# A rule for the order of TensorE's matmuls in a planned kernel: groups that begin whole, and wide runs of at least nine

## The chip, the cores and the metric

The kernel runs on one core of one Trainium2 chip. The metric is the device time of one execution in microseconds (us), median of three runs. The core has a matrix engine (TensorE, PE in the profile; its weight loads are listed as PEld), VectorE (DVE), ScalarE (ACT), GpSimd (POOL) and SyncE (SP), which issues DMAs. Each engine works through its own queue in the order that the program gave it and waits on semaphores for what other engines or DMAs deliver.

## The reference

One decoder layer over 2048 positions of width 1024:

```
h = rms_norm(x, mix_norm_pre)
m = hybrid_mixer(h, ...)                 # attention heads + gated recurrence, then w_out
x = x + rms_norm(m, mix_norm_post)
h = rms_norm(x, mlp_norm_pre)
x = x + rms_norm(squared_relu_mlp(h, w_ff_in, w_ff_out), mlp_norm_post)
```

The attention has 8 heads of 64 columns. Each query attends to three dilated windows, (128, 1), (512, 4) and (2048, 16), and their outputs are weighted by their softmax denominators. The MLP is `relu(h @ w1)**2 @ w2` with a hidden width of 4096. All inputs and outputs are float32.

## The kernel before

**Halves.** The positions are worked on in two halves of 1024. Half 0 goes through projections, first attention, output projection, MLP-in and MLP-out, and half 1 follows. The two overlap in one place that matters here: the attention of half 1 (`attention(..., 1, ...)`, "second attention") runs together with the MLP-out of half 0. The function `interleave` (line 1399) writes the two into one program: between the steps of the attention it puts steps of the MLP-out (`fill`, line 1405), each step three matmuls.

**The MLP-out** (`mlp_out`, line 1183) is a block product in seven partial products `m` (Strassen's scheme), each over 16 blocks `j` and 4 row tiles `t`. Every float32 factor is split into a high and a low part, so a product is three matmuls of 512 columns each (lines 1234 to 1236) into a PSUM tile whose name begins with `o0_` (half 0) or `o1_` (half 1). Their factors come by DMA and are split on ACT and DVE (`part`, line 1310) a few blocks ahead.

**The second attention** (`attention`, line 380) has 48 parts: 8 heads, for each of which two parts A (line 541, the near window) and four parts B (line 601, the dilated ones). A part has three steps, which use PSUM tiles of three kinds:

- scores, twice per part: matmuls into `S1_...` (part A, two query blocks, two matmuls each of 256 columns, line 569) or `SB1_...` (part B, two matmuls of 384 or 512 columns, lines 626 and 627). DVE adds the mask and takes the row minimum (line 426), ACT takes the exponential (line 432).
- turn, twice per part: three or four transposes of 128x128 blocks into `pT1_...` (line 405); ACT and DVE split the result into high and low (lines 56 and 57).
- values: ten matmuls into `oA1_...` (line 593) or eight into `oB1_...` (line 652), of 256 and 128 columns; ACT and DVE fold the result (lines 420 and 421).

At the end of each pair of heads `join` (line 670) weights the two sums: 18 small matmuls into `pst1_...` (lines 684 and 686), then DVE, and stores and loads through DRAM (lines 705, 712, 737). The stores to `smix` feed the output projection of half 1 (tile `m`, lines 869 to 871).

**PSUM** has eight banks; in the second attention the scores share two (`B`), the transposes and the values share two (`T`), and MLP-out holds four (`A` and `O`).

**What sets the order.** The program is traced in the order written, and then `Plan.run` (line 1566) puts every engine's instructions into a new order by a simulation. It finds for each instruction `k` the set `first[k]` of instructions that must come before it: data, reuse of buffers, and, for matmuls into one PSUM tile, the matmul before (lines 1589 to 1592). The class `Machine` (line 1656) then runs the instructions with assumed durations. For every instruction there is a time `need`; for a matmul this is its place in the program, counted in matmul time, and the filler steps get 30 us on top (`FILLER`, line 1454). An engine that is free takes the ready instruction with the smallest `need` (`issue`, line 1791). A matmul counts as ready 0.8 us after the end of the work on another engine that it needs (`SLACK`). So an attention matmul goes ahead of fillers whose program place is less than 30 us before its own, as soon as it is ready, and single matmuls of both kinds can alternate. The orders that come out are fixed in the program (lines 1631 to 1634); the hardware then waits wherever an engine's next instruction isn't ready yet.

Places in the code that the prediction refers to: `first` and `need` as above; `fill` and `FILLER`; the steps scores, turn and values; `join`; the fillers' limit on loads (`edge`, line 1770).

Of the kernel before, what the change touches and what calls it, by code (L numbers as in the profile page):

```python
# [20 lines left out]
TB = 512  # L21
# [1444 lines left out]
LAG = 70.0  # L1466
QUEUED = 2.0
STRICT = 0
ALPHA = 0.6
SLACK = 0.8  # L1470
SLACK2 = 1.0
# [4 lines left out]
class Plan:  # L1476
# [89 lines left out]
    def run(self):  # L1566
        ins = [i for i in self.nc.cur_bb.bb.instructions if i.engine in ENGINES and i.outs]
        eng = [ENGINES[i.engine] for i in ins]
        acc = self.accesses(ins)
        index = {i.name: k for k, i in enumerate(ins)}  # L1570
        first, issued, n = collections.defaultdict(set), {}, len(ins)
        live, group, held = collections.defaultdict(list), {}, collections.defaultdict(set)
        for k, boxes in enumerate(acc):
            for sp, p0, p1, b0, b1, w, name, comb in boxes:
                keep, sp = [], name or sp
                for y in live[sp]:
                    over = y[0] < p1 and p0 < y[1] and y[2] < b1 and b0 < y[3]
                    if over and comb and y[6] and comb[0] == y[6][0]:
                        over = comb[1] < y[6][1] + y[6][2] and y[6][1] < comb[1] + comb[2]
                    if over and (w or y[4]) and y[5] != k:  # L1580
                        first[k].add(y[5])
                    if not (w and over and p0 <= y[0] and y[1] <= p1 and b0 <= y[2] and y[3] <= b1 and y[5] != k
                            and (not comb or comb == y[6])):
                        keep.append(y)
                keep.append((p0, p1, b0, b1, w, k, comb))
                live[sp] = keep
                if name:
                    held[name].add(k)
                if eng[k] == "PE" and w:
                    if name in group:  # L1590
                        first[k].add(group[name])
                    group[name] = k

        def after(k, a):
            nonlocal n
            issued[n] = set(a)
            first[k].add(n)
            n += 1

        for a, b in self.behind:  # L1600
            if a in index and b in index:
                after(index[a], [index[b]])

        rows = []
        for tag, seq in self.taken.items():
            for a, t in seq:
                for k in held[t]:
                    if k != a and any(x[5] and x[6] == t for x in acc[k]):
                        after(k, [a])
            for (a, _), (b, _) in zip(seq, seq[1:]):  # L1610
                if a != b:
                    after(b, [a])
                    if eng[a] != eng[b]:
                        rows.append((a, b))
        guards = []
        for rec in self.pools:
            if rec[1] is not None:
                continue
            old = [r for r in rec[5] if r[4][0] < rec[4][1] and rec[4][0] < r[4][1]]
            if not old:  # L1620
                continue
            guards.append((set().union(*(self.uses[id(r)] for r in old)), set(self.uses[id(rec)])))
            was = [(self.range[t], t) for r in old for tag in self.tags[id(r)] for _, t in self.taken[tag]]
            for tag in self.tags[id(rec)]:
                for k, t in self.taken[tag][:self.slots[tag]]:
                    b0, b1 = self.range[t]
                    for (c0, c1), u in was:
                        if c0 < b1 and b0 < c1:
                            first[k] |= held[u]
        order = Machine(ins, eng, acc, first, issued, self.taken, self.slots, held, guards, self.shift).run()  # L1630
        info = mybir.DependencyInfo(mybir.DependencyClass.NoSync, mybir.DependencyReason.DATA)
        for seq in order.values():
            for a, b in zip(seq, seq[1:]):
                self.tc.add_manual_dep(ins[b], ins[a].name, info, reason="plan")
        for a, b in rows:
            self.tc.add_manual_dep(ins[b], ins[a].name, info, reason="plan")
# [19 lines left out]
class Machine:  # L1656


    def __init__(self, ins, eng, acc, first, issued, taken, slots, held, guards, shift):
# [72 lines left out]
        self.waiting = dict.fromkeys(self.ready, 0.0)  # L1732
        self.lock, self.table, self.far = 0.0, 0, []
        self.done = [False] * n
        self.pe = [k for k in range(n) if eng[k] == "PE"]
        self.front = 0
        self.events, self.ticket, self.now = [], 0, 0.0
# [40 lines left out]
    def hurry(self, k, need):  # L1778
        stack = [k]
        while stack:  # L1780
# [7 lines left out]
                    self.poke(self.eng[k])  # L1788
            stack += self.wait_for[k]

    def issue(self, e):
        self.asked[e] = False
        if self.free[e] > self.now:
            return self.poke(e)
        if sum(self.waiting.values()) > BACKLOG and e in ("SP", "POOL") and isinstance(self.ins[self.ready[e][0][1]], mybir.InstDMACopy) if self.ready[e] else False:
            return
        while self.ready[e]:
            _, k = heapq.heappop(self.ready[e])
            if self.started[k]:
                continue  # L1800
            marks = {g for g in (*self.taint[k], *self.own[k], *self.colour[e]) if self.guard[g][3][0]}
            stop = next((g for g in marks if self.guard[g][2][e]), None)
            if stop is None:
                stop = next((g for g in self.own[k] if self.guard[g][3][0] > STRICT), None)
            if stop is None:
                break
            self.stash[stop, e].append(k)
            for j in self.guard[stop][1]:
                if self.eng[j] == e and not self.started[j]:
                    self.hurry(j, self.need[k])  # L1810
        else:
            return
        self.started[k] = True
        self.taint[k] = self.colour[e] = marks
        for g, (old, seen, count, left) in enumerate(self.guard):
            if k in seen:
                count[e] -= 1
                left[0] -= k in old
                if not count[e] or not left[0]:
                    for x in [e] if left[0] else self.ready:  # L1820
                        for j in self.stash.pop((g, x), ()):
                            heapq.heappush(self.ready[x], (self.need[j], j))
                            self.poke(x)
        self.order[e].append(k)
        i, t = self.ins[k], max(self.free[e], self.now - 0.03)
        self.start[k] = t
        for g in self.gates[k]:
            self.closed[g] -= 1
            self.taint[g] |= self.taint[k]
            if not self.closed[g]:  # L1830
                self.finish(g, None)
        if isinstance(i, mybir.InstDMACopy):
            wait, work = self.transfer(k)
            self.waiting[e] += work
            self.free[e] = t + (0.53 if e == "POOL" else 0.55 if 0.3 < work < 0.83 or 1.9 < work < 2.3 else 0.37)
            self.at(self.free[e] + wait, self.arrive, k, work)
        else:
            hold, last = self.cost(k)
            if e == "PE":
                self.done[k] = True  # L1840
                while self.front < len(self.pe) and self.done[self.pe[self.front]]:
                    self.front += 1
                while self.far and self.far[0][0] <= self.edge():
                    x = heapq.heappop(self.far)
                    heapq.heappush(self.ready[self.eng[x[1]]], x)
                    self.poke(self.eng[x[1]])
                self.at(t, self.finish, k, True)
            if e == "ACT" and (table := TABLES.get(str(getattr(i, "func", None)))) is not None and table != self.table:
                self.table = table
                t += 1.3  # L1850
            if e in ("DVE", "POOL") and self.shared(k):
                t0 = max(t, self.lock)
                self.lock = t0 + (last - 0.1 if e == "POOL" else hold - 0.05)
                t = t0
            self.free[e] = t + hold
            self.at(t + last, self.finish, k, False if e == "PE" else None)
        self.poke(e)
# [92 lines left out]
def trunk(tc, x, xT, g1, g2, g3, g4, w_in, conv_w, conv_b, w_r, b_r, w_i, b_i, lam, w_out, w1, w2,  # L1950
# [11 lines left out]
    with (  # L1962
# [49 lines left out]
        with contextlib.ExitStack() as st:  # L2012
# [55 lines left out]
            with sb("at0", "right") as pa:  # L2068
                attend = attention(tc, pa, lambda k, n: bank(place[k][0], n), cst, scr, 0, mask_a, mask_b, pa)
                run(ORDER)  # L2070
# [163 lines left out]
```

## Time and profile before

| | us |
|---|---|
| median of three runs | 2177.39 |
| lowest and highest | 2175.86, 2177.82 |
| the profiled execution | 2174.38 |
| its span, first to last instruction | 2172.6 |
| TensorE busy | 2136.3 (98% of the span) |
| VectorE busy | 1520.6 (70%) |
| ScalarE busy | 1229.1 (57%) |
| GpSimd busy | 482.5 (22%) |

The profile is of one execution. An instruction's busy time on TensorE is listed from the start of its reading to a modelled end, so busy times of neighbouring matmuls overlap; how long a matmul holds the engine is read from one start to the next. A line such as `L405 PE MATMUL pT<-ident,sm ... x4` stands for four instructions in a row of line 405 that write the tile `pT` and read `ident` and `sm`; buffer numbers are left out of the names, so `o` is any `o0_...` or `o1_...` tile and `pT_B` a transposed tile of a part B. `128*128 128x256` says rows and columns of the array in use, and partitions by columns of the data that stream through it. What stands in brackets is the idle time of the engine before the instruction and what ended it. The granted clock is the share of TensorE's clock pulses that the throttle let pass.

### The profile page before, as it was taken

Reading aid. Unit: us, or ns where it says so; the run is one execution under the profiler, and the core shown is the slowest. Engines: PE = TensorE matmul, PEld = TensorE weight load, DVE = VectorE, ACT = ScalarE, POOL = GpSimd, SP = SyncE. Lnnn points to the kernel's source line nnn. Section 1 sums busy time; section 2 is a strip of 40 time slices with the busy share of each in tenths; the row PEclk is TensorE's granted clock in tenths of the full one; section 3 lists DMA queues with packets and bytes.
Section 4 is the critical chain, followed back from the end, with each engine's and each line's share of the span. In section 5 each row is a group of like instructions: output and inputs, shape, how many; then the busy total and the mean of one; then the engine's idle time right before and its main releaser. Section 6 shows DMA issues by size and latency. Waiting matters only on the chain.

```text
span 2172.6 us, 30852 instructions
## 1 busy us (share of the span) xinstructions
PE 2136.3 (98%) x10264; PEld 1754.5 (81%) x10264; DVE 1520.6 (70%) x2893; ACT 1229.1 (57%) x2486; POOL 482.5 (22%) x556
## 2 busy tenths in 40 slices
PE   8999999999999999999999999999999999999998
PEld 6777888777788788888888888878788888888887
DVE  7858667858878777775776868787766565664456
ACT  7537566634554655554766667764455555654442
POOL 4652534567523001000010101113100000000003
PEclk9999999999999999999999999999999999999999
DMA  7557686358765667779777785796634444866665
GB/s 249 174 157 212 199 259 194 120 185 296 222 229 180 247 255 296 280 271 356 240 227 222 231 259 170 229 297 192 230 129 174 146 153 146 327 203 193 193 192 183
DMA packets 224548, 473.51 MB, mean 218 GB/s; under 512 B 23476, under 2 KB 79572, under 8 KB 218116
## 3 DMA queue, kind: packets, MB, share of 16 engines
q1 hardware_dynamic: 195572, 337.52, 48.7%
q0 software_dynamic: 28816, 134.01, 17.3%
q8 instruction: 81, 1.33, 0.3%
q14 instruction: 79, 0.65, 0.1%
HBM read 337.09 MB, written 151.13 MB: 225 GB/s over the span
## 4 chain that ended last, share of the span: by engine, by line
PE 84%; DVE 6%; ACT 5%; issue 2%; POOL 2%; DMA 1%; DVEq 0%; POOLq 0%; ACTq 0%; SPq 0%
PE o L1234 9%; PE o L1236 9%; PE o L1235 9%; PE za L1085 5%; PE za L1086 5%; PE za L1084 5%; PE z L210 4%; PE z L209 4%; PE z L208 4%; PE m L871 3%; PE m L870 3%; PE m L869 3%; PE zc L1084 3%; PE zc L1085 3%; PE zc L1086 3%; PE oB L652 2%
## 5 line engine op out<-in xcount | busy, mean ns | idle before, releaser
L208 PE MATMUL z<-hH,wH 128*128 128x512 f32 x640 | 254.6, 399 | 7.3 <-ACT wH L56 5.1
L209 PE MATMUL z<-hL,wH 128*128 128x512 f32 x640 | 256.8, 402 | 0.4 <-DVE hL L183 0.4
L210 PE MATMUL z<-hH,wL 128*128 128x512 f32 x640 | 254.3, 399 | 0.0
L208 PEld LDWEIGHTS z<-hH,wH 128*128 128x128 f32 x640 | 120.7, 189 | 35.0 <-ACT wH L56 5.6
L209 PEld LDWEIGHTS z<-hL,wH 128*128 128x128 f32 x640 | 120.8, 189 | 28.5 <-issue 3.8
L210 PEld LDWEIGHTS z<-hH,wL 128*128 128x128 f32 x640 | 120.8, 189 | 25.7 <-issue 3.6
L57 POOL TENSOR_TENSOR wL<-wraw,wH 128x512 fp32r<-128x512 f32 x70 | 96.0, 1384 | 55.9 <-ACT wH L56 54.4
L1089 ACT ACTIVATE sq<-sq 128x512 f32<-128x512 f32 x93 | 58.8, 632 | 76.6 <-DVE sq L1093 76.6
L1149 POOL DMA_DIRECT2D sa<-sq x31 | 16.5, 532 | 376.6 <-ACT sq L1090 363.7
L432 ACT ACTIVATE smB<-smB,stB 128x128 f32<-128x128 f32 (+3 forms) x128 | 71.5, 560 | 41.5 <-DVE stB L426 41.2
L432 ACT ACTIVATE sm<-sm,stA 128x256 f32<-128x256 f32 (+1 forms) x128 | 63.4, 497 | 53.6 <-DVE stA L426 53.4
L57 DVE TENSOR_TENSOR tlB<-pT_B,thB 128x384 fp32r<-128x384 f32 x96 | 57.1, 598 | 30.4 <-ACT thB L56 27.6
L1090 ACT ACTIVATE sq<-sq 128x512 f32<-128x512 f32 x124 | 76.9, 630 | 2.6
L56 ACT CAST wH<-wraw 128x512 fp32r<-128x512 f32 (+1 forms) x84 | 47.8, 596 | 43.9 <-PE z L209 28.0
L1268 POOL TENSOR_TENSOR y<-y,g4b 128x512 f32<-128x512 f32 x8 | 12.4, 1573 | 257.1 <-ACT junk_y L86 257.1
L426 DVE CUSTOM_DVE_ANT_0 smB<-SB,mask_b 128x128 f32<-128x128 f32 (+3 forms) x128 | 59.3, 485 | 7.3 <-PE SB L627 5.8
L426 DVE CUSTOM_DVE_ANT_0 sm<-S,mask_a 128x256 f32<-128x256 f32 (+1 forms) x128 | 47.5, 408 | 23.4 <-PE S L569 23.3
L405 PE MATMUL pT_B<-ident,smB 128*128 128x128 f32 x320 | 59.9, 277 | 1.7 <-DVE tlB L57 0.9
L240 DVE TENSOR_TENSOR zn<-z,bc 128x512 f32<-128x512 f32 x32 | 22.0, 688 | 54.4 <-PE z L210 52.0
L56 ACT CAST thB<-pT_B 128x384 fp32r<-128x384 f32 x96 | 48.9, 511 | 18.9 <-PE pT_B L405 15.1
L322 DVE SCALAR_TENSOR_TENSOR xc<-xr,cw,xc 128x512 f32<-128x512 f32 x48 | 52.9, 1110 | 6.0 <-POOL xc L319 5.6
L57 POOL TENSOR_TENSOR zl<-zn,zh 128x512 fp32r<-128x512 f32 x28 | 39.4, 1408 | 61.9 <-ACT zh L56 52.5
(607 smaller groups left out, 7075.9 us busy)
## 6 DMA issues: line engine op xcount, KB each, us to landing
sa<-as POOLq DMA_DIRECT2D x31, 1024.0 KB, 6.8
w1r<-in_dram SPq DMA_DIRECT2D x56, 512.0 KB, 4.3
sa<-sq POOLq DMA_DIRECT2D x31, 768.0 KB, 4.0
wraw<-in_dram SPq DMA_DIRECT2D x76, 256.0 KB, 3.5
place<-in_dram SPq DMA_DIRECT2D x14, 1024.0 KB, 6.7
sb<-place POOLq DMA_DIRECT2D x14, 1024.0 KB, 4.2
kh<-sk SPq DMA_DIRECT2D x24, 512.0 KB, 5.1
kl<-sk SPq DMA_DIRECT2D x24, 512.0 KB, 6.8
```

The lines of the kernel that those rows point to most:

```text
L57: (lo_eng or nc.vector).tensor_tensor(out=lo, in0=src, in1=f32(hi), op=ALU.subtract))
L208: pe.matmul(z, hi[:, k, :], hh, start=(k == 0), stop=False)
L209: pe.matmul(z, hi[:, k, :], hl, start=False, stop=False)
L210: pe.matmul(z, lo[:, k, :], hh, start=False, stop=(k == KT - 1))
L426: v.tensor_tensor_reduce(out=sm[:, c0:c0 + w], in0=sp[:, c0:c0 + w], in1=mask[:, mask.shape[-1] - w:], scale=1.0, scalar=3.0e38, op0=ALU.a ...
L432: s.activation(out=sm[:, c0:c0 + w], in_=sm[:, c0:c0 + w], func=AF.Exp, scale=-1.0, bias=st[:, 0, u, cols[j]:cols[j] + 1], accum_out=st[:, ...
L1084: pe.matmul(o, hi[:, k], bh[:, k], start=start and k == 0, stop=False, skip_group_check=True)
L1085: pe.matmul(o, hi[:, k], bl[:, k], start=False, stop=False, skip_group_check=True)
L1086: pe.matmul(o, lo[:, k], bh[:, k], start=False, stop=k == KH - 1, skip_group_check=True)
L1234: pe.matmul(o, ah[:, ts], bh, start=fresh and j == 0, stop=False, skip_group_check=True)
L1235: pe.matmul(o, ah[:, ts], bl, start=False, stop=False, skip_group_check=True)
L1236: pe.matmul(o, al[:, ts], bh, start=False, stop=j == NJ - 1, skip_group_check=True)
```

## The change

Two rules are added to the planner; no instruction of the kernel is added, removed or altered, only their order on the engines can differ.

1. `TOGETHER`: in `Plan.run`, for a run of consecutive matmuls in the program that write one PSUM tile whose name begins with `pT1`, `S1`, `SB1`, `oA1` or `oB1` (all of the second attention), everything that any of them depends on, and that isn't itself one of the group's matmuls, is added to what the first of them depends on.
2. `RUN`: in `Machine.issue`, matmuls of 512 columns into a tile whose name begins with `o` are `wide`. After a wide matmul has gone, a matmul that isn't wide goes only when nine wide ones have gone in a row, or when no wide one is ready. The test for blocked instructions is moved into a function of its own, `blocked`, so that it can be asked for the wide candidates too.

```diff
+TOGETHER = ("pT1", "S1", "SB1", "oA1", "oB1")
+RUN = 9
@@ Plan.run
+        head, last = None, None
+        for k in range(len(ins)):
+            if eng[k] != "PE":
+                continue
+            name = next(x[6] for x in acc[k] if x[5])
+            if head is not None and name == last:
+                first[head] |= {j for j in first[k] if eng[j] != "PE" or j < head}
+            else:
+                head = k if name.startswith(TOGETHER) else None
+            last = name
@@ Machine.__init__
+        self.run_length = 0
+        self.wide = [e == "PE" and np.prod([c for _, c in list(i.outs[0].bass_ap.ap)[1:]]) == TB and x[0][6].startswith("o")
+                     for i, e, x in zip(ins, eng, ([y for y in a if y[5]] or [(0,) * 7] for a in acc))]
@@ Machine
+    def blocked(self, e, k):
+        marks = {g for g in (*self.taint[k], *self.own[k], *self.colour[e]) if self.guard[g][3][0]}
+        stop = next((g for g in marks if self.guard[g][2][e]), None)
+        if stop is None:
+            stop = next((g for g in self.own[k] if self.guard[g][3][0] > STRICT), None)
+        return marks, stop
@@ Machine.issue
-            marks = {g for g in (*self.taint[k], *self.own[k], *self.colour[e]) if self.guard[g][3][0]}
-            stop = next((g for g in marks if self.guard[g][2][e]), None)
-            if stop is None:
-                stop = next((g for g in self.own[k] if self.guard[g][3][0] > STRICT), None)
+            if e == "PE" and 0 < self.run_length < RUN and not self.wide[k]:
+                more = min((x for x in self.ready[e] if self.wide[x[1]] and not self.started[x[1]]
+                            and self.blocked(e, x[1])[1] is None), default=None)
+                if more:
+                    heapq.heappush(self.ready[e], (self.need[k], k))
+                    k = more[1]
+            marks, stop = self.blocked(e, k)
...
             if e == "PE":
+                self.run_length = self.run_length + 1 if self.wide[k] else 0
```

## The prediction

> **What bounds the kernel now.** I read the page first, then the windows view over the stretch that the change touches, then TensorE's timeline matmul by matmul inside it. Columns of a windows row: the stretch, its length, busy time and count of PE, PEld, DVE, ACT (and POOL), the granted clock, DMA share, GB/s.
>
> ```profile
> span 2172.6 us, 30852 instructions
> ```
> ```profile
> 1005.00:1398.00 393.00, 390.25 (x2193) 327.96 (x2192) 289.99 (x662) 268.89 (x607) 42.01 (x74) 1.00 0.77 232
> 1005.00:1398.00 393.00, 322.40 (x1096) 196.58 (x1097) 2.74 (x4) 8.97 (x16) 1.00 0.77 232
> 1010.00:1060.00 50.00, 48.08 (x256) 39.34 (x255) 27.01 (x67) 26.85 (x67) 1.59 (x3) 1.00 0.88 297
> 1900.00:1950.00 50.00, 50.00 (x222) 41.36 (x221) 32.24 (x51) 29.77 (x52) 0.00 (x0) 1.00 0.66 205
> ```
>
> TensorE is the bound. The second attention stands between 1005 and 1398 us: 2193 matmuls, of which 1096 are MLP-output matmuls of 512 columns (second row, the tile o alone). I call these the wide ones and the rest narrow. PE idles 2.75 us of the 393, and 1.92 of that lies between 1010 and 1060. The clock is granted in full. So the change can win only what order costs: stalls, and time between two starts beyond what the matmul itself takes. The last row is the measure: wide ones alone show 222 in 50 us, two of them cut by the edges, so 50 / 220 = 0.227 from start to start.
>
> I counted the places where a wide one is followed by a narrow one: 388 in these 393 us (the first just ahead of the row at 1008.55 below, the last the pst at 1396.82), and 211 of these wide runs are a single matmul. With nine in a row there would be about 1096 / 9 = 122. The question is what one such change of kind costs.
>
> **What an interruption costs.** First column of the timeline: the start. Starts are what counts; the second column overlaps with the next matmul.
>
> ```profile
> 1119.56 0.60 PE L405 MATMUL pT<-ident,sm 128*128 128x128 f32 x4
> 1119.92 0.48 PE L1235 MATMUL o<-b_10L,a_10H 128*128 128x512 f32 x1
> 1120.24 0.40 PE L1236 MATMUL o<-b_10H,a_10L 128*128 128x512 f32 x1
> 1120.47 0.28 PE L593 MATMUL oA<-tlA,va 128*128 128x256 f32 x1
> 1120.60 0.22 PE L593 MATMUL oA<-thA,va 128*128 128x128 f32 x1
> 1120.66 0.27 PE L593 MATMUL oA<-tlA,va 128*128 128x128 f32 x1
> 1120.77 0.33 PE L593 MATMUL oA<-thA,va 128*128 128x256 f32 x1
> 1120.94 0.28 PE L593 MATMUL oA<-tlA,va 128*128 128x256 f32 x1
> ```
> ```profile
> 1057.75 0.27 PE L405 MATMUL pT_B<-ident,smB 128*128 128x128 f32 x1
> 1057.77 0.48 PE L1235 MATMUL o<-b_12L,a_12H 128*128 128x512 f32 x1
> 1058.09 0.38 PE L405 MATMUL pT_B<-ident,smB 128*128 128x128 f32 x2
> ...
> 1058.89 0.40 PE L1235 MATMUL o<-b_12L,a_12H 128*128 128x512 f32 x1
> ```
>
> *Transposes.* Four together: busy 0.60 against 0.27 for one, so (0.60 - 0.27) / 3 = 0.11 each. Four and the wide one behind take 1120.24 - 1119.56 = 0.68, against 4 x 0.11 + 0.227 = 0.667: 0.01 lost. A tile of four broken into 1, 2 and 1 (at the dots stand a wide one, the last transpose and a wide one): 1058.89 - 1057.75 = 1.14 for four transposes and three wide ones, against 0.44 + 0.681 = 1.12: 0.02 lost. The wide one behind a transpose looks slow (0.32 to the next start), but the transpose before it looks just as much too quick (0.02): the sum is unharmed. So joining a tile's transposes saves 0.00 to 0.01. There are 96 such tiles (16 parts A with 2 and 32 parts B with 2): at most 1 us; I take **-0.5**.
>
> *The 128-column value matmuls.* A pair side by side: 1120.60, 1120.66, 1120.77, 1120.94. The first costs 0.06, the second 0.11, the 256-column one behind it 0.17, where two 256-column ones start 0.12 apart elsewhere in the run (1120.47 to the next is 0.13). That is about 0.10 lost for a pair. With a wide one between the two, part of the loss has cover. The code makes 64 pairs (two in each of 16 oA groups, one in each of 32 oB runs), and I count 12 that are broken now; the change joins these. Bounds: 0 and 12 x 0.10 = 1.2; I take **+0.6**, the middle. The Trainium skill, TensorE: Matmul & The Clock Gate, LDWEIGHTS, speaks against the change here: a weight load takes the 128 columns over 1.2, an estimate of 107 ns, more than a 128-column matmul lasts, so each one that no wide one covers loses about 48 ns; by it the term is 12 x 0.096 = 1.15, the upper end.
>
> *After a change of kind.*
>
> ```profile
> 1008.55 0.40 PE L1234 MATMUL o<-b,a 128*128 128x512 f32 x1
> ...
> 1027.01 0.28 PE L569 MATMUL S<-kl,qa 128*128 128x256 f32 x1
> ...
> 1027.60 0.28 PE L569 MATMUL S<-kl,qa 128*128 128x256 f32 x1
> 1028.49 0.36 PE L569 MATMUL S<-kh,qa 128*128 128x256 f32 x1 [0.61 <-DVE stA L426]
> ...
> 1102.23 0.40 PE L1235 MATMUL o<-b_6L,a_6H 128*128 128x512 f32 x1
> ...
> 1104.08 0.62 PE L1234 MATMUL o<-b_7H,a_7H 128*128 128x512 f32 x2
> ```
>
> A run of 81 wide ones (1008.55 to 1027.01) has 0.2279 from start to start. The run that begins at 1102.23 has eight starts in 1.85 us, 0.231. So a wide one costs about 4 ns more for the first eight or so of a run, and a run of nine is over when that ends. If all 1096 fell to the long run's rate: 1096 x 0.0035 = -3.8. If the first nine keep it in full and singles had less of it, about +1.2 (122 runs x 0.01). I take **0**: the rows show the loss inside a run just as long as the change asks for. The Trainium skill, Perfetto Trace Analysis, Matmul Optimizations, speaks for the change: matmuls back to back in batches matter, since the engine scales its power with use. Every row above has the clock at 1.00, so by that rule there is nothing left to gain here.
>
> *Joins.* The four pst tiles are not in the list of groups, but with wide ones in batches fewer of these should stand inside them.
>
> ```profile
> 1112.95 0.41 PE L684 MATMUL pst<-sel,sa 128*16 128x32 f32 x8
> ...
> 1114.81 0.27 PE L405 MATMUL pT<-ident,sm 128*128 128x128 f32 x1
> ...
> 1396.82 0.41 PE L684 MATMUL pst<-sel,sa 128*16 128x32 f32 x8
> ...
> 1397.74 0.49 PE L1234 MATMUL o<-b_11H,a_11H 128*128 128x512 f32 x1
> ```
>
> The 18 matmuls of one tile take 0.92 in one piece (1396.82 to 1397.74), and 1.86 with two wide ones in between (to 1114.81), that is 1.86 - 0.454 = 1.41: 0.49 more. Three tiles are cut like that. Bounds 0 and -1.5; I take **-0.7**.
>
> *Waits.* A group that begins when all its inputs are there can't stall in its middle, and nine wide ones (9 x 0.227 = 2.04 us) give inputs time. Of the 2.75 us of idle PE, 0.83 lie outside the stretch 1010 to 1060: -0.8 at most there, I take **-0.5**. In that stretch no wide matmul is ready from 1027.01 to 1036 (the timeline has none), so RUN does nothing, and the chain of scores, softmax and transposes sets the pace: 0.89 us pass from 1027.60 to 1028.49 on stA. There a head that waits for the last of several inputs starts later than the first matmul did. Behind it on PE stands all the rest of the attention, with no cover. Bounds: -1.9 (all that idle gone) and +3 (0.9 more, as at 1028.49, for about three groups); I take **+0.6**, well inside.
>
> Sum: -0.5 + 0.6 + 0 - 0.7 - 0.5 + 0.6 = **-0.5 us**. DVE and ACT get the same instructions; at 290 and 269 of 393 us they have room. No DMA is added. The rule of nine also holds where the second half's wide ones begin, near 1858; PE has work there either way (the row of 1900), so I put that at nothing. The profiled execution took 2174.38 (span 2172.6 and 1.8 around it), the median of the runs is 2177.39; on the median the forecast is **2176.9**, no change.
>
> **Rivals.**
> *A: batches pay in full (faster).* The settling goes (-3.8), so do the idle times (-2.8) and the cuts in the joins (-1.0): -7.6, **2169.8**. For it: 388 changes of kind are many. Against it: broken and unbroken transposes cost the same to 0.01 us, and a run of nine is no longer than the settling.
>
> *B: the attention falls behind and the fillers run out (slower).*
>
> ```profile
> 1036.18 0.28 PE L593 MATMUL oA<-tlA,va 128*128 128x128 f32 x1
> ...
> 1055.95 0.28 PE L652 MATMUL oB<-tlB,vb 128*128 128x128 f32 x1
> ```
> ```profile
> 1422.51 0.54 POOL L737 DMA_DIRECT2D smix<-na  x1 [4.03 <-DVE na L736]
> ```
> ```profile
> 1456.13 0.39 PE L869 MATMUL m<-woH,m_0H 128*128 128x512 f32 x1
> ```
>
> Half 0 has 7 x 16 x 4 x 3 = 1344 wide matmuls; 96 come ahead of the attention, 1000 beside its 48 parts (20.8 each), 248 are left at 1398 and last until the next stage's first matmul at 1456.13. These 56 us cover the last join, whose store is issued at 1422.51, and the load and split behind it; I estimate 33 us from the last attention matmul (25 to the store's issue, 8 beyond), 146 wide ones' worth. A part has three dependent steps (first turn, second turn, values). If each waits for a run of nine, 27 wide ones go per part, and the fillers end before the attention does. The cost begins at (1248 - 146) / 48 = 23.0 per part; at 24 the remainder is 96 (22 us) and PE idles 11 us: **2188**. Against it: unhindered, four parts take 19.8 us (1036.18 to 1055.95), 4.9 each, and the mean is 393 / 48 = 8.2, so 3.3 us, one and a half runs of nine, fit into each part for nothing; and values can share a batch with the next part's first turn.
>
> *C: nothing to hold.* If too few wide ones are ready when nine are asked for, the rule lets the narrow one go, and the order is nearly the old one: **2177.4**.
>
> **How the numbers follow.** About 0.2%, 4.4 us, is what a measurement of this kernel can tell from no change. Forecast 0.50 and C 0.08 lie within it: 0.58. A: 0.24 faster. B 0.12, and 0.06 for the upper ends of start-up, pairs and settling together with no gain beside them (+5.4): 0.18 slower. The bounds of the small terms add up to -1 - 3.8 - 1.5 - 0.8 - 1.9 = -9.0 and 1.2 + 1.2 + 3 = +5.4; that all the low ones meet is left out, and the range takes in A and most of B: 2169 to 2187.
>
> **What would show it.** Right: between 1005 and 1398 the same 393 us within 4 at 1.00 clock; about 120 to 180 wide runs instead of 388, transposes unbroken, wide ones still 0.230 to 0.231. A shows as 0.228 there and no idle PE. B shows as idle PE between the last oB and the first m. Start-up wrong: more or less idle PE between 1027 and 1036. The forecast is wrong above all if the new order moves waits outside this stretch, in the stages behind 1398, which no row here can show.

## The result and the profile after

| us | before | after |
|---|---|---|
| median, 18 runs each | 2175.63 | 2179.57 |
| lowest and highest | 2172.19, 2180.91 | 2175.53, 2183.08 |
| the profiled execution | 2174.38 | 2180.44 |
| its last oB, its first m | 1396.1, 1456.1 | 1405.7, 1463.4 |

The ratio of after to before is 1.0016, with a 95% interval of 1.0009 to 1.0024: 3.5 us slower. The two profiled executions lie further apart, 6.1 us, because that of before is 1.25 us under its median and that of after 0.87 over. "Last oB" is the start of the attention's last value matmul, "first m" that of the next stage's first matmul.

The page and the windows view of the changed kernel, for the stretches of the prediction and two that turned out to matter (all matmuls, and in the second row of the windows the tile o alone):

```profile
span 2178.7 us, 30873 instructions
```
```profile
1005.00:1398.00 393.00, 385.50 (x2155) 328.09 (x2154) 286.29 (x657) 266.80 (x604) 42.24 (x74) 1.00 0.77 233
1005.00:1398.00 393.00, 275.00 (x1100) 202.01 (x1099) 2.65 (x4) 8.82 (x16) 1.00 0.77 233
1010.00:1060.00 50.00, 47.21 (x247) 39.08 (x246) 24.74 (x61) 24.60 (x60) 1.53 (x3) 1.00 0.93 317
1360.00:1410.00 50.00, 47.62 (x263) 39.80 (x262) 35.40 (x74) 36.90 (x70) 4.32 (x6) 0.97 0.74 210
1410.00:1460.00 50.00, 46.41 (x197) 37.42 (x196) 38.96 (x65) 29.23 (x51) 8.45 (x13) 0.97 0.97 308
```

The same two late stretches in the kernel before:

```profile
1360.00:1410.00 50.00, 49.58 (x272) 40.96 (x271) 38.14 (x81) 38.66 (x72) 7.43 (x13) 1.00 0.79 225
1410.00:1460.00 50.00, 48.94 (x214) 39.58 (x213) 39.87 (x69) 32.64 (x57) 7.08 (x8) 1.00 0.97 323
```

PE has as many wide matmuls in the 393 us as before (1100 against 1096), but 38 matmuls fewer in all. The last two rows say where PE loses time: it idles 1.96 and 2.53 us more there, and the granted clock, 1.00 before, is 0.97.

For an account of the whole I took every matmul's start from TensorE's timeline between 1004.5 us and the first m, and subtracted what a matmul takes in a row of its own kind (0.227 us for 512 columns, 0.172 for 384, 0.117 for 256, 0.059 for 128, 0.109 for a transpose). What remains I call **time lost**. It rose from 22.6 to 30.0 us, that is by 7.4; behind the first m the execution of the changed kernel was 1.1 us quicker (715.3 us to the end against 716.4), and the rest is where the two stood at 1004 us. The account is thus one of these two executions, and larger than the 3.5 us between the kernels. The pieces of up to 0.15 us fell from 15.6 to 13.6: the order did what it was to do, with 119 wide runs instead of 388. The longer ones rose from 7.0 to 16.4, at these places:

- 1004 to 1045, the start-up: 2.99 to 3.03 us.
- 1045 to 1250: 1.07 to 3.82 us, two of them alone 0.82 and 1.42, at scores that wait for DVE.
- 1250 to 1355: 0.78 to 0.
- 1355 to the last oB: 0.77 to 4.08.
- behind the last oB: 1.39 to 5.48.

**The first place.** ScalarE's timeline of the changed kernel, then TensorE's:

```profile
1384.03 0.61 ACT L1319 CAST b_10H<-b_10L 128x512 fp32r<-128x512 f32 x1
1386.12 0.62 ACT L1319 CAST a_11H<-a_11L 128x512 fp32r<-128x512 f32 x1 [1.48 <-DMA a_11L<-sa]
1386.65 0.47 ACT L56 CAST thB<-pT_B 128x384 fp32r<-128x384 f32 x1
```
```profile
1385.25 0.40 PE L1236 MATMUL o<-b_9H,a_9L 128*128 128x512 f32 x1
1387.99 1.12 PE L405 MATMUL pT_B<-ident,smB 128*128 128x128 f32 x4 [2.35 <-DVE tlB L57]
...
1389.76 0.63 PE L1234 MATMUL o<-b_9H,a_9H 128*128 128x512 f32 x1
1390.18 0.63 PE L1235 MATMUL o<-b_9L,a_9H 128*128 128x512 f32 x1
1390.61 0.63 PE L1236 MATMUL o<-b_9H,a_9L 128*128 128x512 f32 x1
1391.04 0.48 PE L1234 MATMUL o<-b_9H,a_9H 128*128 128x512 f32 x1
```

The transposes need a bank that DVE's tlB frees, tlB needs ScalarE's thB, and thB stands in ScalarE's queue behind a filler's cast, which waits for a load (a_11L, 6.81 us from issue to landing). PE waits 2.35 us. Then look at the starts: 1389.76, 1390.18, 1390.61, each 0.427 apart and not 0.227. After the wait TensorE runs at about half its rate for a while (the last section says how long).

**The second place.** TensorE again:

```profile
1428.52 0.39 PE L1236 MATMUL o<-b_4H,a_4L 128*128 128x512 f32 x1
1431.66 1.24 PE L1234 MATMUL o<-b_5H,a_5H 128*128 128x512 f32 x3 [2.75 <-ACT b_5H L1319]
1432.70 0.63 PE L1235 MATMUL o<-b_5L,a_5H 128*128 128x512 f32 x1
...
1434.83 0.63 PE L1236 MATMUL o<-b_5H,a_5L 128*128 128x512 f32 x1
1435.26 0.56 PE L1234 MATMUL o<-b_5H,a_5H 128*128 128x512 f32 x1
1435.65 0.40 PE L1235 MATMUL o<-b_5L,a_5H 128*128 128x512 f32 x1
```

ScalarE's cast of b_5H stands behind that of a_5H, which had waited 4.49 us for the load a_5L. SyncE's timeline shows the issues (at the dots stand three more r loads, issued up to 1420.93):

```profile
1418.43 0.42 SPq L1227 DMA_DIRECT2D r<-sa  x1
...
1421.66 0.46 SPq L1227 DMA_DIRECT2D a_5L<-sa  x1
```

and the list of DMA issues the time from issue to landing (count, size of one, median us), first of the changed kernel, then of the kernel before:

```profile
co<-sco POOLq DMA_DIRECT2D x8, 128.0 KB, 4.8
r<-sa SPq DMA_DIRECT2D x2, 256.0 KB, 8.8
...
a_3L<-sa SPq DMA_DIRECT2D x1, 256.0 KB, 2.9
...
a_5L<-sa SPq DMA_DIRECT2D x1, 256.0 KB, 8.6
```
```profile
r<-sa SPq DMA_DIRECT2D x2, 256.0 KB, 6.6
...
a_3L<-sa SPq DMA_DIRECT2D x1, 256.0 KB, 8.1
...
a_5L<-sa SPq DMA_DIRECT2D x1, 256.0 KB, 5.7
```

The four r loads are factors of the last blocks of MLP-out, fetched ahead; they are issued at a fixed filler step. The eight co loads belong to the last join, so they move with the end of the attention. Before, GpSimd issued them from 1407.9 to 1411.5, and the first r load came 3.8 us later. After, they are issued from 1415.4 to 1419.0, and the first r load goes out 0.6 us before the last of them. The load a_5L, one of the next that PE needs, is issued behind both and takes 8.55 us instead of 5.69. So I read the second place as a meeting of two streams of transfers, brought about by the later end of the attention. The Trainium skill, DMA: Bandwidth & Descriptors, Queues, rings and completion order, says that a DMA engine takes packets from its rows in turn and works through one row in ring order. By that, a_5L shares the engines with co and stands behind r, which agrees with 5.69 against 8.55 here.

The kernel before had a collision too, a smaller one: its co loads met a_3L, which took 8.07 us there and 2.87 in the changed kernel. It cost PE 1.17 us beyond the matmul (1418.74 to 1420.13, TensorE's timeline of the kernel before):

```profile
1418.74 0.39 PE L1236 MATMUL o<-b_2H,a_2L 128*128 128x512 f32 x1
1420.13 0.96 PE L1234 MATMUL o<-b_3H,a_3H 128*128 128x512 f32 x3 [1.01 <-ACT b_3H L1319]
```

### The profile page after: what moved, and what is told of

Its sections match the earlier page's. It is cut to its first block, busy times and chain, and to the rows that moved or that the text cites. A ratio compares the mean times of both kernels' runs of the same rounds, so it can differ in the third digit from the quotient of the medians.

```text
span 2178.7 us, 30873 instructions
## 1 busy us (share of the span) xinstructions
PE 2133.8 (98%) x10264; PEld 1757.0 (81%) x10264; DVE 1515.5 (70%) x2893; ACT 1227.9 (56%) x2486; POOL 482.5 (22%) x556
## 4 chain that ended last, share of the span: by engine, by line
PE 84%; DVE 6%; ACT 3%; issue 2%; POOL 2%; DMA 2%; SPq 0%; DVEq 0%; POOLq 0%; ACTq 0%
PE o L1234 9%; PE o L1236 9%; PE o L1235 9%; PE za L1085 5%; PE za L1086 5%; PE za L1084 5%; PE z L210 4%; PE z L209 4%; PE z L208 4%; PE m L871 3%; PE m L869 3%; PE m L870 3%; PE zc L1085 2%; PE zc L1086 2%; PE zc L1084 2%; PE oB L652 2%
## 5 line engine op out<-in xcount | busy, mean ns | idle before, releaser
L56 ACT CAST wH<-wraw 128x512 fp32r<-128x512 f32 (+1 forms) x84 | 47.5, 595 | 43.9 <-PE z L209 24.2
L405 PE MATMUL pT_B<-ident,smB 128*128 128x128 f32 x320 | 55.3, 279 | 4.3 <-DVE tlB L57 3.4
```

## The experiments

Ratios are to the kernel before, with 95% intervals. Intervals are about 0.0009 to either side, 2 us, so the profile often says more than the ratio. The times of the last oB and the first m are to be read with care: all kernels issue the same matmuls up to 1004 us, but their profiled executions reach the last of these at 1003.4 to 1006.5 us. Time lost is counted from 1004.5 us on and hardly feels that.

### One rule at a time

Groups alone:

```diff
-RUN = 9
+RUN = 0
```

> TOGETHER alone, no batches (RUN = 0). In the changed kernel the starts lost to order fell, but PE stands still longer: 2.5 us ahead of the transposes at 1388, 1.0 and 2.9 us ahead of wide matmuls at 1425 and 1431, each with slow matmuls behind. Theory 1: the batches hold the attention back, its last matmul comes 9 us later, and its last join then meets the fillers' loads; TOGETHER has no part in it: last oB within 3 us of the kernel before, ratio 0.998 to 1.001. Theory 2: heads that wait for all their inputs make the attention late: last oB 5 us or more later, ratio 1.001 to 1.003. Theory 3: any new order scatters a few long waits by chance: ratio anywhere from 0.998 to 1.003, long waits in other places.

Measured: 2174.35 us, ratio 0.9993 (0.9984 to 1.0002). The last oB comes at 1399.1 and the first m at 1455.3; 330 wide runs; time lost 22.4.

Batches alone:

```diff
-TOGETHER = ("pT1", "S1", "SB1", "oA1", "oB1")
+TOGETHER = ("none",)
```

> RUN = 9 alone, no groups. Theory 1: last oB 5 us or more later than in the kernel before, long waits near 1390 to 1435 as in the changed kernel, ratio 1.001 to 1.003. Theory 2: last oB within 3 us, ratio 0.998 to 1.001. Theory 3: ratio anywhere from 0.998 to 1.003, waits in places that neither kernel has.

Measured: 2171.54 us, ratio 0.9984 (0.9976 to 0.9993), faster than both kernels. The last oB comes at 1396.5, the first m at 1452.8; 119 wide runs as in the changed kernel; time lost 20.1. The windows view:

```profile
1360.00:1410.00 50.00, 49.29 (x265) 40.87 (x264) 39.46 (x81) 33.60 (x66) 9.48 (x16) 1.00 0.81 238
1410.00:1460.00 50.00, 49.26 (x217) 40.30 (x216) 40.20 (x75) 34.28 (x62) 6.68 (x6) 1.00 0.90 304
```

So neither rule is slow by itself. That the batches hold the attention back falls in its plain form, and so does that the groups do: in this program the loss comes with the two together. Theory 3, that any new order scatters a few long waits by chance, fits both ratios and isn't ruled out.

### Less of the batches, with both rules on

```diff
-            if e == "PE" and 0 < self.run_length < RUN and not self.wide[k]:
+            if e == "PE" and self.wides < EARLY and 0 < self.run_length < RUN and not self.wide[k]:
...
+                self.wides += self.wide[k]
```

with EARLY = 800, so that the rule holds for the first 800 wide matmuls only.

> Both rules, but RUN holds only until 800 wide matmuls have gone (about 1300 us), so that the end of the attention runs free. Theory 1: the attention catches up, last oB near 1397, no wait over 1.5 us between 1380 and 1435; the order saves about 2 us of starts before that, ratio 0.997 to 1.000. Theory 2: nothing gained, 1.001 to 1.002. Theory 3: anywhere from 0.997 to 1.003.

Measured: 2176.93 us, ratio 1.0005 (0.9996 to 1.0014); last oB 1402.5, first m 1458.8, time lost 23.3. The loss of 1.42 us near 1072 is still there, the largest late ones are 0.91 and 1.25. Theory 1 had asked for a last oB near 1397 and a ratio of at most 1.000 and gets neither, though no late wait is over 1.5 us; the ratio fits Theory 3 alone.

Batches of three (`RUN = 3`):

> Both rules with RUN = 3: a held group waits at most 0.7 us instead of 2.0. Theory 1: the attention is late by a third as much or less, last oB within 4 us of the kernel before, ratio 0.998 to 1.001. Theory 2: as the changed kernel, 1.001 to 1.002. Theory 3: anywhere from 0.998 to 1.003.

Measured: 2175.04 us, ratio 0.9999 (0.9991 to 1.0008); last oB 1398.6, first m 1458.7, time lost 25.0. This is what Theory 1 said of a shorter batch, and Theory 3 allows it too.

In each of these four PE loses time in the same two stretches, from 1355 to the last oB and from 1412 to 1440, but not the same amount and not at the same instruction. From this I formed Theory 4: the loss is made where the attention's transfers and casts meet those of the fillers, plus the half-rate stretch behind each long wait.

### The order of TensorE kept, six instructions elsewhere moved

These edits come after the planner. TensorE's order is that of the changed kernel, instruction by instruction. In the first, `later` (its definition stands at the dots) puts SyncE's four r loads behind the load of b_6L:

```diff
         order = Machine(ins, eng, acc, first, issued, self.taken, self.slots, held, guards, self.shift).run()
...
+        later("SP", ("r0_4_12", "r0_4_13"), "b0_4_6L")
```

> Every engine keeps the order that it has in the changed kernel, but for SyncE, where the four loads r<-sa, r<-sb that are issued at 1418.43 to 1420.93 now stand behind the loads a_5L, b_5L, a_6L, b_6L. Theory 4 (the loss is two collisions and what the clock does after each): in the changed kernel TensorE waits 1.0 us at 1424.6 and 2.9 us at 1428.5 for b_4H and b_5H, and then runs some ten matmuls 0.2 us late each. With the loads out of the way a_5L is issued some 3 us sooner: the 2.9 us fall to under 1 us, the half-rate stretch behind it goes, the first m moves from 1463.4 to 1458.5 to 1460.5, and the ratio to the kernel before is 0.9993 to 1.0005 where the changed kernel had 1.0016. Rival (the late attention costs by its mere lateness, and a wait taken away comes back at the next place): the first m stays within 1.5 us of 1463.4 and the ratio is 1.0010 to 1.0020.

Measured: 2178.31 us, ratio 1.0007 (0.9998 to 1.0016); first m 1460.2. The issue list and the windows view of this run:

```profile
a_5L<-sa SPq DMA_DIRECT2D x1, 256.0 KB, 7.1
```
```profile
1360.00:1410.00 50.00, 47.77 (x264) 39.77 (x263) 35.76 (x73) 37.19 (x70) 4.33 (x6) 0.97 0.75 210
1410.00:1460.00 50.00, 49.01 (x212) 39.04 (x211) 41.51 (x70) 30.68 (x54) 9.91 (x14) 1.00 0.98 322
```

The 2.91 us lost at a_5 are down to 0.26, the half-rate stretch behind it is gone (0.97 to 1.00) and PE is busy 2.6 us more between 1410 and 1460. The stretch 1360 to 1410, which the edit doesn't touch, is as bad as it was. The first m came 3.2 us sooner (3.8 counted from the last matmul that all kernels have in common), as Theory 4 said; the ratio is just above its range and below the rival's. The run doesn't tell apart two things: a_5L is issued 1.7 us sooner, no longer behind four other issues (1419.94 instead of 1421.66), and it takes 1.5 us less (7.07 instead of 8.55). No run moves the co loads.

In the second, `swap` exchanges an instruction with the next one of its engine, so that thB goes ahead of the cast of a_11H and tlB ahead of the subtraction of a_11L:

```diff
+        swap("ACT", "a0_7_11H")
+        swap("DVE", "a0_7_11L")
```

> Every engine keeps the order that it has in the changed kernel, but for two pairs of neighbours: on ScalarE the cast thB<-pT_B now stands ahead of a_11H<-a_11L (1386.12 and 1386.65), and on VectorE tlB ahead of a_11L<-a_11L,a_11H. Theory 4: thB no longer stands behind a cast that waits for a DMA, so TensorE's wait of 2.35 us at 1385.25 falls to 0.3 to 0.8 us and the five matmuls behind it are no longer 0.2 to 0.35 us late: the last oB moves from 1405.7 to 1402.0 to 1403.5, and the ratio is 0.9999 to 1.0009. The loss at 1424 to 1435 stays (it may shrink by up to 1 us, as the join comes sooner). Rival (the wait comes back at the next place): last oB stays within 1 us of 1405.7, ratio 1.0010 to 1.0020.

Measured: 2179.99 us, ratio 1.0014 (1.0005 to 1.0023); last oB 1404.4, first m 1460.8. In TensorE's timeline of this run the wait at the first place is 0.20 us, and a part of it returns at the next transposes:

```profile
1387.40 0.66 PE L405 MATMUL pT_B<-ident,smB 128*128 128x128 f32 x4 [0.20 <-DVE tlB L57]
1400.61 0.66 PE L405 MATMUL pT_B<-ident,smB 128*128 128x128 f32 x4 [0.62 <-DVE tlB L57]
...
1429.09 0.98 PE L1234 MATMUL o<-b_5H,a_5H 128*128 128x512 f32 x3 [2.59 <-ACT b_5H L1319]
```

The last oB came 1.3 us sooner, not the 2.2 to 3.7 expected; but this execution reached the last common matmul 1.3 us later than that of the changed kernel (1005.77 against 1004.44), so the stretch itself is 2.6 us shorter, inside the range, and up to the first m it is 3.9 us shorter. The whole time shows no gain, and the ratio is the rival's: the run is inconclusive. In the profiled execution a half-rate stretch at 1582 us (last section) took back 2.7 us behind the first m.

Both edits together:

> The edits of the last two runs together; TensorE's own order is still that of the changed kernel. Theory 4: the two gains add to 5.5 to 8 us, the first m comes at 1455.5 to 1458, and the ratio is 0.9978 to 0.9995, that is, the changed order of TensorE is as good as or better than the one before, and the whole loss was in the order of six transfers and casts on other engines. Rival (lateness itself costs): the first m stays above 1460 and the ratio is above 1.0005.

Measured: 2176.12 us, ratio 1.0001 (0.9992 to 1.0010); first m 1458.1, 5.3 us sooner than in the changed kernel, and 5.9 counted from the last common matmul, where 5.5 to 8 were expected. Windows and TensorE's timeline of this run:

```profile
1360.00:1410.00 50.00, 49.06 (x275) 40.58 (x274) 37.80 (x80) 38.50 (x72) 4.33 (x6) 1.00 0.75 220
1410.00:1460.00 50.00, 48.35 (x210) 38.45 (x209) 39.93 (x66) 30.97 (x54) 10.21 (x14) 1.00 0.99 326
```
```profile
1423.98 0.97 PE L1234 MATMUL o<-b_4H,a_4H 128*128 128x512 f32 x3 [1.22 <-ACT b_4H L1319]
```

With the same order of TensorE, six instructions in another place on three other queues bring the ratio from 1.0016 back to 1.0001 (the intervals, 1.0009 to 1.0024 and 0.9992 to 1.0010, hardly overlap). The clock is at 1.00 in both stretches. That is most of the loss but not the gain that the batches alone have: the 3.5 us lost from 1045 to 1250 are still there, and PE now waits 1.2 us for b_4H. Theory 4 asked for 0.9978 to 0.9995 and got part of it; the rival asked for a first m above 1460 and a ratio above 1.0005 and got neither. So most of the loss is shown to lie with these six instructions, under an order of TensorE that made their places matter.

The r loads moved in the same way in the kernel with batches alone:

> The kernel with the batches alone (no groups), its engines' orders kept but for the four r loads on SyncE, which stand behind a_5L to b_6L as in the run of the later loads. It waited 0.90 us at 1421.6 for such a load, and its ratio was 0.9984. Theory 4: that wait goes below 0.3 us, the first m comes 0.5 to 1 us before 1452.8, the ratio is 0.9977 to 0.9984. Rival (there is no collision there, the transfers being busy anyway): the wait is the same or moves to a_7, the ratio stays at 0.9984 within 0.0004.

Measured: 2172.77 us, ratio 0.9984 (0.9976 to 0.9993), as without the edit; first m 1455.6, 1.1 us later than without it if counted from the last common matmul. The loss of 0.90 us became three of 0.43, 0.39 and 0.50. In the kernel without the edit the last co load is issued 4.8 us ahead of the first r load, so there was no meeting to remove. The rival was right.

### Which groups, and how long a batch

Batches of six (`RUN = 6`) with all groups:

> Both rules, RUN = 6. Theory 5 (the two rules delay the attention together, and the loss grows with the length of a batch: time lost between 1004 and the first m was 22.4 us with RUN = 0, 25.0 with 3, 30.0 with 9): lost time 26.5 to 29 us, last oB between 1399 and 1405, ratio 1.0003 to 1.0014. Theory 4 in its plain form (how badly the two collisions come out is chance of the plan): any ratio from 0.9985 to 1.0020, not between the neighbours; the waits at 1360 to 1390 and at 1416 to 1436 make up the difference.

Measured: 2179.08 us, ratio 1.0014 (1.0004 to 1.0025); last oB 1404.2, time lost 27.1, all as Theory 5 said; Theory 4 in its plain form allows them too. Its second place, from TensorE's timeline:

```profile
1425.12 0.96 PE L1234 MATMUL o<-b_4H,a_4H 128*128 128x512 f32 x3 [1.73 <-ACT b_4H L1319]
...
1429.93 0.97 PE L1234 MATMUL o<-b_5H,a_5H 128*128 128x512 f32 x3 [1.75 <-ACT b_5H L1319]
```

`RUN = 9`, and only pT as a group (`TOGETHER = ("pT1",)`):

> RUN = 9, and of the groups only the transposes into pT wait for their last input. Theory 5: the delay of the pT groups is the one on the attention's chain (pT, cast, subtract, oA or oB), so this has most of the loss: lost time above 25 us, ratio 1.0003 to 1.0016. Rival (it is S and SB, whose pairs wait for a bank of PSUM: waits of 0.82 and 1.42 us at 1052 and 1070 that neither rule alone has): lost time 19 to 22 us as with the batches alone (20.1), ratio 0.9982 to 0.9992, and no wait over 0.7 us between 1045 and 1250.

Measured: 2175.36 us, ratio 1.0002 (0.9993 to 1.0011); time lost 19.8. The two measures disagree: the time lost is the rival's, the ratio lies in neither range, next to that of Theory 5. The profiled execution took 2173.31, 2 us under the median.

`RUN = 9`, and all groups but pT (`TOGETHER = ("S1", "SB1", "oA1", "oB1")`):

> RUN = 9, and the groups S, SB, oA, oB wait for their last input, pT does not. Theory 5 with pT as the culprit: lost time 19 to 22 us, ratio 0.9982 to 0.9992. Rival (S and SB): the waits at SB or S over 0.7 us between 1045 and 1250 are there, lost time above 25 us, ratio 1.0003 to 1.0016. If both runs lie near 0.9985, it takes all groups together.

Measured: 2173.07 us, ratio 0.9992 (0.9983 to 1.0000); time lost 20.2; no wait over 0.7 us between 1045 and 1250. By the time lost, then, neither pT alone nor the other four kinds without it bring the loss about. By the ratio pT may have a part in it (1.0002 against 0.9984 with no groups), and that stays open.

Batches of six alone:

> Batches alone, six long instead of nine (no groups). If the gain of the batches alone (ratio 0.9984) is due to fewer changes between narrow and wide matmuls, this lies between: the small start losses at 14.0 to 15.0 us, ratio 0.9984 to 0.9996. If that gain was chance of the plan, the ratio may be anywhere from 0.9985 to 1.0015.

Measured: 2176.21 us, ratio 1.0008 (0.9999 to 1.0017); time lost 23.1, of it 14.9 in small pieces. The gain of batches alone at nine, 0.9984, isn't a property of batches as such: at six the small losses behave as expected, and losses of 2.18 and 2.45 us in the two stretches, none of them over 1.6 us in one piece, eat the gain.

### All together

"Wide ahead" counts the wide matmuls of half 0 that the order puts ahead of the last oB; "gap" is the time from the issue of the last co load to that of the first r load; "flight" is a_5L from issue to landing; "second place" is the sum of PE's losses over 0.15 us from 1412 to 1440, half-rate matmuls among them. The first eleven rows are sorted by the gap; in the run marked * and in the two after it the r loads were moved by hand.

| kernel | ratio | wide ahead | gap | flight | second place | time lost |
|---|---|---|---|---|---|---|
| after | 1.0016 | 1120 | -0.6 | 8.55 | 5.48 | 30.0 |
| casts swapped | 1.0014 | 1120 | -0.4 | 8.22 | 4.15 | 26.1 |
| both, RUN 6 | 1.0014 | 1117 | 0.5 | 9.05 | 3.80 | 27.1 |
| groups but pT, RUN 9 | 0.9992 | 1115 | 1.7 | 7.00 | 1.86 | 20.2 |
| RUN 6 alone | 1.0008 | 1111 | 2.5 | 7.52 | 2.45 | 23.1 |
| before | 1 | 1093 | 3.8 | 5.69 | 1.39 | 22.6 |
| group pT, RUN 9 | 1.0002 | 1103 | 4.4 | 6.02 | 0.49 | 19.8 |
| both, early | 1.0005 | 1103 | 4.6 | 6.75 | 1.25 | 23.3 |
| RUN 9 alone | 0.9984 | 1103 | 4.8 | 6.25 | 0.90 | 20.1 |
| groups alone | 0.9993 | 1103 | 5.2 | 5.59 | 0.91 | 22.4 |
| both, RUN 3 | 0.9999 | 1096 | 5.3 | 5.57 | 2.92 | 25.0 |
| loads later * | 1.0007 | 1120 | 4.7 | 7.07 | 1.04 | 26.3 |
| both edits | 1.0001 | 1120 | 4.8 | 7.68 | 2.13 | 24.2 |
| RUN 9 alone, loads later | 0.9984 | 1103 | 9.5 | 3.46 | 1.32 | 21.2 |

What the reader is to see: the two rules together, with batches of six or nine throughout, put 1117 to 1120 wide matmuls ahead of the last oB, up to 27 more than before (27 x 0.227 = 6.1 us). With that the gap closes, a_5L takes 8 to 9 us, and the second place costs 3.8 to 5.5 us. The count alone doesn't do it: the groups without pT have 1115, a gap of 1.7, and 1.86 us there. One kernel stands outside, batches of three, with a gap of 5.3 and still 2.92 us there. That both streams slow a_5L shows in four flights: 3.46 us with neither in its way (RUN 9 alone, loads later), 5.69 behind r alone (before), 7.07 beside co alone (loads later) and 8.55 with both (after). Why the two rules hold the attention back only when both are on isn't settled: by the time lost neither pT nor the other groups do it alone with the batches. That a group which has waited for its last input then waits for the batch too is my reading, and only argued.

## Why the prediction was wrong

It said 2176.9 and no change; the ratio says 3.5 us slower. The time is within the range, the direction isn't the forecast one. That the time came within 3 us is partly luck: the three runs that the forecast started from lay 1.8 us above the median of eighteen. By its steps:

**Small terms: right in kind, too small.** Transposes, pairs, settling and joins were to give -0.5 + 0.6 + 0 - 0.7 = -0.6 us. The small pieces of time lost fell by 2.0. Wide matmuls side by side lost 6.7 us instead of 10.1, and the changes from one kind of tile to another, fewer by more than half, came to -2.8 instead of 0.8. Pairs of scores side by side, now twice as many, lost 4.6 instead of 1.0, and the other narrow pairs 5.1 instead of 3.8. Settling was thus set too low, at 0 (rival A had it near its size), and narrow matmuls that no longer have a wide one between them pay most of it back; for the scores among them the sum had no term. Transposes now come in 100 pieces instead of 160, and the three cut join tiles went from 1.41 us each to 1.00, 1.2 us in all where the term had 0.7.

**Start-up: right, and small.** PE's four waits there were to cost 0.6 us more. They come to 2.02 us in the changed kernel's timeline (0.48 + 0.26 + 0.66 + 0.62) and 1.66 before (0.61 + 0.28 + 0.44 + 0.33): 0.36 more. By time lost it is 0.04.

**Waits outside the start-up: wrong, and this is the step that failed.** It was -0.5 us, bounded by -0.8 and 0, on the reason that a group that begins whole can't stall in its middle and that nine wide ones give inputs time. Long losses between the start-up and the last oB rose from 2.6 to 7.9 us, so the term was +5.3. The bound was the error: it counted only waits that could go away and left out those that a changed order makes. A stall in the middle became a stall at the head, where the queue behind it waits just the same (2.35 us at pT_B, 1.25 at the scores near 1072).

**Rival B: the right sign, another mechanism.** The attention did fall behind, the last oB by 9.6 us. But the fillers did not run out. PE waited for the wide matmuls' own factors, whose loads came late: behind the r loads in SyncE's queue, and beside the transfers of a late join. B's point of decision, 23.0 wide ones per part, was not reached: the mean rose from 1000 / 48 = 20.8 by 27 / 48, to 21.4. The price came all the same.

**Behind 1398 nothing moves: wrong, and named as the risk.** The forecast had warned of waits behind 1398. They came, 4.1 us more behind the last oB (5.48 against 1.39), where the sum had nothing: as the attention ended later, the join's transfers moved onto the r loads and a_5L. A row for it did stand in the profile of before: the 1.17 us that PE lost at 1418.7, where the join's transfers already met a filler's load, showed a place with no slack.

**The clock.** The prediction took the clock at 1.00 as given, since every row showed it. The long waits took it away: behind the two of them, matmuls at half rate lost 2.9 of the 9.4 us by which the long losses grew (5.3 + 4.1). Over whole runs, the granted clock was 0.9976 on the mean of the eighteen runs of the changed kernel, and 0.9982 in 99 later runs of the kernel before. If every pulse withheld costs its time, that makes an estimate of 0.0006 x 2175 = 1.3 us of the 3.5.

## What to carry to other kernels

When a rule changes the order of the bounding engine, look for the transfers that are tied to the one stream and not to the other, and work out where they meet once one stream comes later; bound the waits by what the new order can make, not only by the waits that are there. Where two rules come in one change, measure each alone: here RUN alone (0.9984) beats both kernels, and the two together are slower than either. And a gain of 0.2% from one planned order need not hold for the next: RUN = 6 alone gave 1.0008.

## What the hardware showed unexpectedly

**Short idle times can halve TensorE's rate, and not in every execution.** All four idle times of 1.98 us or more that PE had between 1360 and 1435 in the fourteen profiled executions (1.98, 2.35, 2.59, 2.75) were followed by wide matmuls 0.427 us apart. At shorter ones it varies. Here is the same point of the program in the kernel before and in the changed one, from TensorE's timelines:

```profile
1574.65 0.73 PE L1084 MATMUL za<-hHT,f_6H 128*128 128x512 f32 x2 [1.70 <-ACT hHT L56]
1576.73 0.80 PE L1085 MATMUL za<-hLT,f_6H 128*128 128x512 f32 x1 [1.35 <-DVE hLT L57]
1577.32 0.63 PE L1086 MATMUL za<-hHT,f_6L 128*128 128x512 f32 x1
1577.75 0.63 PE L1084 MATMUL za<-hHT,f_6H 128*128 128x512 f32 x1
```
```profile
1581.94 0.73 PE L1084 MATMUL za<-hHT,f_6H 128*128 128x512 f32 x2 [1.67 <-ACT hHT L56]
1584.02 0.50 PE L1085 MATMUL za<-hLT,f_6H 128*128 128x512 f32 x1 [1.35 <-DVE hLT L57]
1584.36 0.39 PE L1086 MATMUL za<-hHT,f_6L 128*128 128x512 f32 x1
1584.59 0.40 PE L1084 MATMUL za<-hHT,f_6H 128*128 128x512 f32 x1
```

The idle times are the same (1.70 and 1.35, 1.67 and 1.35), but the first execution goes on at 0.43 us per matmul and the second at 0.23. Of the fourteen executions nine have the slow stretch at this point; after two idle times of 1.03 and 0.77 us near 723, four of fourteen have one.

The record of the granted clock says what differs. Where it falls, between 60 us and the end of the work, it falls to 0.50 for 3.41 us or for twice that, and in one execution the starts of these pieces lie whole multiples of 3.413 us apart (1387.82 and 1432.19 in the changed kernel: 44.37 = 13 x 3.413). So there is a grid of windows, and its phase differs from execution to execution. Two neighbouring windows of the kernel before, then two of the changed one, at the point above; PE's busy time is the first figure behind the length, the clock the third from the end:

```profile
1572.97:1576.38 3.41, 0.73 (x2) 0.30 (x2) 3.41 (x7) 3.41 (x8) 0.00 (x0) 1.00 0.47 156
1576.38:1579.80 3.42, 3.07 (x7) 2.49 (x8) 3.42 (x7) 3.39 (x7) 0.00 (x0) 0.50 0.00 0
```
```profile
1578.96:1582.38 3.42, 1.75 (x8) 1.05 (x6) 3.42 (x7) 3.23 (x7) 0.00 (x0) 1.00 0.69 238
1582.38:1585.79 3.41, 2.06 (x10) 1.47 (x9) 3.41 (x7) 3.41 (x8) 0.00 (x0) 1.00 0.15 57
```

Before, the two idle times fall into one window, 2.68 us together, and the next window has half the clock. After, an edge of the grid parts them, 1.67 and 1.35, and the clock stays. From 60 us on, in all fourteen executions, each of the 16 full-clock windows with 1.80 us of idle PE or more was followed by one at 0.50; of the 18 with 1.50 to 1.74 us one was. The Trainium skill, TensorE: Matmul & The Clock Gate, What's actually happening, says that half rate follows an idle window of about 3.4 us and that the window runs freely, so that its phase differs from run to run. The phase and the length of the window agree with these rows; a whole window of idle time wasn't needed here, as 1.80 us in it were enough each time.

This is much of what spreads the times of one kernel. In the eighteen runs of the changed kernel the spans average 2175.2 us where the granted clock was 0.999 (six runs) and 2180.0 where it was 0.996 (four); the two at 0.998 average 2179.6, so it isn't all. A change that makes idle times near 2 us can pay twice, and a single execution can't tell 2 us of gain from the clock.
